# Weight blocks of two tiles: all high-part products before the low-part products

## Chip, cores and metric

The kernel runs on one core of one Trainium2 chip. The metric is the time of one execution on the device in microseconds (us); lower is better, and the output must match the reference.

## The reference

One layer of a hybrid network on 256 tokens of width 2048, with fp32 inputs. `rmsnorm(x)` is multiplied by `w_in` (7440 columns). Of the result, 4112 columns feed a gated delta rule (causal convolution, chunks, a triangular solve) and 3328 feed an RWKV-7 recurrence. Their outputs go through `w_out` and are added to `h`. Then come a cross-attention over 256 memory tokens and a squared-ReLU MLP of hidden width 8192:

```python
h = x
u = rmsnorm(h, mix_norm_w[l]);  p = u @ w_in[l]
o_dn = deltanet_group(p[..., :DN_COLS], ...)
o_rw = rwkv7_group(p[..., DN_COLS:], ...)
h = h + jnp.concatenate([o_dn, o_rw], axis=-1) @ w_out[l]
h = h + memory_cross_attention(rmsnorm(h, xa_norm_w[l]), rmsnorm(mem, mem_norm_w[l]), ...)
h = h + squared_relu_mlp(rmsnorm(h, ffn_norm_w[l]), ffn_w1[l], ffn_w2[l])
return rmsnorm(h, final_norm_w)
```

## The kernel before

Every large product is made from fp32 operands that are split in two parts, a high part rounded to fp32r and the rest as a low part. Three of the four partial products are summed in PSUM: high by high, low activation by high weight, high activation by low weight.

`weights` (L228) loads one block of weights of 512 KB into a `raw` tile (4 buffers) through the SP queue, and splits it: for each of the two 128-row tiles of the block, ScalarE casts the high part `whi` (L239) and VectorE subtracts for the low part `wlo` (L240, recorded as L110, the line of the helper `tt`). `whi` and `wlo` have three buffers each (`WB = 3`), one tile to a buffer. This code has a raised priority (`tc.high_priority(3000)`), so that it is put ahead of other work.

`gemm` (L244) makes a result of 256 tokens by 512 columns. It holds two accumulators of one PSUM bank each, one for each half of the tokens (`m` = 0, 1); the tag "g" has three banks in all. It loops over the blocks `kb` of two weight tiles `q`. For each tile it issues six matmuls of 512 columns, the activations being the stationary operand: for each `m` the high activation by `whi` (L254) and the low activation by `whi` (L255), then for each `m` the high activation by `wlo` (L257). After the last tile `evac` empties each bank: for the MLP and `w_out` on VectorE, for `w_in` half on ScalarE and half on VectorE.

`gemm` is called for 14 groups of `w_in` columns, for `wk` and `wv` (16 tiles each), 8 times for `w_out` (8 tiles), 4 times for `wo` (4 tiles) and 15 times for `w2` (16 tiles): 576 tiles. `gemm_T` (L262) makes the transposed products with `wq` and `w1`; it uses the same `weights` and buffers, with matmuls at L278 and L281. `gemm_rows` (L205) makes the last 512 columns of `w2`, one token half after the other, with buffers of its own; it keeps all its matmuls of one half in one bank.

The order of the instructions on each engine is not that of the program alone. `TileContext(nc, schedule_with_timeline_sim=True)` plans it: instructions are taken by priority (their place in the program, raised where the code says so) as their inputs and buffers become free on a modelled time line. Until about 700 us the many small fp32 matmuls of the two recurrences and of the attention are mixed among those of `gemm` in this way; from then on the MLP is `gemm_T` and `gemm` in turn.

Of the kernel before, what the change touches and what calls it, by code (L numbers as in the profile page):

```python
# [22 lines left out]
KB = 2  # L23
# [81 lines left out]
def body(ctx, tc, I, out, dbg=None, upto=99):  # L105
    nc = tc.nc
    V, A, G, T = nc.vector, nc.scalar, nc.gpsimd, nc.tensor
# [37 lines left out]
    def bank(tag=None):  # L145

        if tag is None:
            tag = ("s0", "s1", "x")[cnt[0] % 3 if stream[0] is None else stream[0]]
        return ps.tile([P, 512], F32, tag=tag, bufs={"g": 3, "x": 1}.get(tag, 2), name=nm("ps_" + tag))
# [78 lines left out]
    def weights(src, a, b, parts):  # L228

        with tc.high_priority(3000):  # L230
            raw = wp.tile([P, a, b], F32, tag="raw", name=nm("raw"))
            nc.sync.dma_start(out=raw, in_=src)
            res = []
            n = a // parts
            for q in range(parts):
                hi = wp.tile([P, n, b], F32R, tag="whi", bufs=WB, name=nm("whi"))
                lo = wp.tile([P, n, b], F32R, tag="wlo", bufs=WB, name=nm("wlo"))
                w = raw[:, q * n:(q + 1) * n]
                A.copy(hi, w)  # L239
                tt(lo, w, hi.bitcast(F32), ALU.subtract)  # L240
                res += [(hi[:, i], lo[:, i]) for i in range(n)]
        return res

    def gemm(lhs, wblk, n, evac, kbs=None):  # L244

        acc = [bank("g") for _ in range(2)]
        kbs = list(kbs if kbs is not None else range(NKT // KB))
        for kb in kbs:
            w = weights(wblk[kb], KB, n, KB)
            for q in range(KB):  # L250
                first, last = kb == kbs[0] and q == 0, kb == kbs[-1] and q == KB - 1
                for m in range(2):
                    xh, xl = lhs(kb * KB + q, m)
                    T.matmul(acc[m][:, :n], lhsT=xh, rhs=w[q][0], start=first, stop=False)  # L254
                    T.matmul(acc[m][:, :n], lhsT=xl, rhs=w[q][0], start=False, stop=False)  # L255
                for m in range(2):
                    T.matmul(acc[m][:, :n], lhsT=lhs(kb * KB + q, m)[0], rhs=w[q][1], start=False, stop=last)  # L257
                    if last:
                        evac(m, acc[m][:, :n])
# [132 lines left out]
    acc = []  # L392
# [6 lines left out]
    with tc.manual_schedule(engines={mybir.EngineType.Activation, mybir.EngineType.DVE}):  # L399
        for kb in range(NKT // KB):  # L400
# [5 lines left out]
            for m in range(2):  # L406
                for q in range(KB):
                    first, last = kb == 0 and q == 0, kb == NKT // KB - 1 and q == KB - 1
                    xh, xo = xl(kb * KB + q, m)
# [3 lines left out]
        for j in range(4):  # L413
# [4 lines left out]
            for m in range(2):  # L418
                T.matmul(ssb[:, 4 * m + j:4 * m + j + 1], lhsT=xs[:, m * P:(m + 1) * P], rhs=ones[:, 0:1],
                         start=True, stop=True)  # L420
# [363 lines left out]
    def win_group():  # L784
        pt = pts()
        gemm(xl, I["w_in"][gi[0]], NB, evac_tok(rx, pt))
        gi[0] += 1
        return pt
# [233 lines left out]
    ptk = pts()  # L1022
    mT = mem_T(lx, "lx")
    gemm(mT, I["wk"][0], NB, evac_tok(rm, ptk))
    to_T(ptk, KT)
    gemm(mT, I["wv"][0], NB, evac_tok(rm, [Vm[:, 0], Vm[:, 1]]))
    for j in range(2):
        split_out(j)
# [92 lines left out]
    for gcol in range(4):  # L1121
        gemm(lambda kt, m: tuple(t[:, m * P:(m + 1) * P] for t in oa[kt]), I["wo"][gcol], NB, add_h(gcol),
             kbs=range(2))
# [70 lines left out]
    for ch in range(4):  # L1194
# [16 lines left out]
        for gcol in range(4):  # L1211
            kbs = range(8 * ch, 8 * ch + 8)
# [26 lines left out]
```

## Time and profile before

| what | us |
|---|---|
| median of 3 runs (1423.86 to 1430.27) | 1428.85 |
| the profiled execution | 1427.91 |
| its span, first to last instruction | 1426.2 |
| TensorE matmul busy (99% of the span) | 1407.6 |
| weight loads busy (82%) | 1172.1 |
| VectorE busy (66%) | 945.7 |
| ScalarE busy (54%) | 776.2 |

PE is TensorE's matmuls, PEld its weight loads, DVE VectorE, ACT ScalarE, POOL GpSimd, SPq and ACTq the queues that issue DMAs. A name like `ps_g<-whi,xhl` says which tile is written from which. A matmul's row is longer than the distance to the next one's start, because matmuls are pipelined and their ends are modelled: a PE that shows no idle time may still have waited a little, and the distance from start to start tells how fast it really goes.

### The profile page before, as it was taken

Reading aid. Unit: us, or ns where it says so; the run is one execution under the profiler, and the core shown is the slowest. Engines: PE = TensorE matmul, PEld = TensorE weight load, DVE = VectorE, ACT = ScalarE, POOL = GpSimd, SP = SyncE. Lnnn points to the kernel's source line nnn. Section 1 sums busy time; section 2 is a strip of 40 time slices with the busy share of each in tenths; the row PEclk is TensorE's granted clock in tenths of the full one; section 3 lists DMA queues with packets and bytes.
Section 4 is the critical chain, followed back from the end, with each engine's and each line's share of the span. In section 5 each row is a group of like instructions: output and inputs, shape, how many; then the busy total and the mean of one; then the engine's idle time right before and its main releaser. Section 6 shows DMA issues by size and latency. Waiting matters only on the chain.

```text
span 1426.2 us, 22860 instructions
## 1 busy us (share of the span) xinstructions
PE 1407.6 (99%) x8308; PEld 1172.1 (82%) x8308; DVE 945.7 (66%) x1788; ACT 776.2 (54%) x1476; POOL 53.0 (4%) x66
## 2 busy tenths in 40 slices
PE   9999999999999999999999999999999999999997
PEld 7877888788887878888788888888888888888886
DVE  7748563858688685766776555665556665566664
ACT  7655554455556454556765544555445544455553
POOL 0010001010010000000000000000000000000000
PEclk9999999999999999999999999999999999999999
DMA  7444443454358455555465566555665556655564
GB/s 272 160 154 142 137 130 106 136 195 140 105 186 238 141 170 173 177 177 178 140 200 189 187 191 198 186 187 192 192 193 191 189 188 194 194 185 188 192 192 148
DMA packets 90114, 250.80 MB, mean 176 GB/s; under 512 B 20609, under 2 KB 29329, under 8 KB 89617
## 3 DMA queue, kind: packets, MB, share of 16 engines
q1 hardware_dynamic: 69728, 241.86, 52.3%
q10 hardware_dynamic: 19920, 6.42, 1.9%
q8 instruction: 65, 1.06, 0.3%
q0 software_dynamic: 352, 1.06, 0.2%
q14 instruction: 49, 0.39, 0.1%
HBM read 242.62 MB, written 6.69 MB: 175 GB/s over the span
## 4 chain that ended last, share of the span: by engine, by line
PE 51%; issue 0%; ACT 0%; DVE 0%; POOLq 0%; POOL 0%
PE ps_g L278 17%; PE ps_g L281 9%; PE ps_g L255 8%; PE ps_g L254 8%; PE ps_g L257 8%; PE ps_g L223 0%; PE ps_g L225 0%; PE ps_g L224 0%; PE ps_x L320 0%; PE ps_s L320 0%; PE ps_s L1112 0%; ACT h L122 0%; ACT junk L122 0%; ACT whi L239 0%; POOLq L1235 0%
## 5 line engine op out<-in xcount | busy, mean ns | idle before, releaser
L110 DVE TENSOR_TENSOR wlo<-raw,whi 128x512 fp32r<-128x512 f32 x848 | 582.1, 691 | 366.6 <-ACT whi L239 314.2
L239 ACT CAST whi<-raw 128x512 fp32r<-128x512 f32 x848 | 524.0, 621 | 485.7 <-DVE wlo L110 202.6
L278 PE MATMUL ps_g<-hhl,whi 128*128 128x512 f32 x1088 | 297.3, 395 | 0.0
L254 PE MATMUL ps_g<-whi,xhl 128*128 128x512 f32 x512 | 207.4, 405 | 0.9 <-ACT whi L239 0.6
L278 PEld LDWEIGHTS ps_g<-hhl,whi 128*128 128x128 f32 x1088 | 186.7, 189 | 25.5
L255 PE MATMUL ps_g<-whi,xhl 128*128 128x512 f32 x512 | 204.1, 399 | 0.0
L254 PE MATMUL ps_g<-whi,fhi 128*128 128x512 f32 x480 | 186.8, 389 | 0.0
L255 PE MATMUL ps_g<-whi,flo 128*128 128x512 f32 x480 | 186.8, 389 | 0.0
L281 PEld LDWEIGHTS ps_g<-hhl,wlo 128*128 128x128 f32 x1088 | 166.3, 189 | 22.6
L281 PE MATMUL ps_g<-hhl,wlo 128*128 128x256 f32 x1088 | 172.9, 281 | 0.0
L257 PE MATMUL ps_g<-wlo,xhl 128*128 128x512 f32 x512 | 170.4, 405 | 2.1 <-DVE wlo L110 2.1
L257 PE MATMUL ps_g<-wlo,fhi 128*128 128x512 f32 x480 | 151.5, 389 | 0.0
L254 PEld LDWEIGHTS ps_g<-whi,xhl 128*128 128x128 f32 x512 | 97.2, 190 | 23.6 <-issue 1.7
L255 PEld LDWEIGHTS ps_g<-whi,xhl 128*128 128x128 f32 x512 | 97.1, 190 | 21.1 <-issue 2.2
L257 PEld LDWEIGHTS ps_g<-wlo,xhl 128*128 128x128 f32 x512 | 94.3, 190 | 23.8 <-DVE wlo L110 4.5
L255 PEld LDWEIGHTS ps_g<-whi,flo 128*128 128x128 f32 x480 | 90.1, 188 | 18.8
L257 PEld LDWEIGHTS ps_g<-wlo,fhi 128*128 128x128 f32 x480 | 90.1, 188 | 18.7
L254 PEld LDWEIGHTS ps_g<-whi,fhi 128*128 128x128 f32 x480 | 90.1, 188 | 18.5
L113 DVE SCALAR_TENSOR_TENSOR cy<-ps_x,colt,cy 128x255 f32<-128x255 f32 (+2 forms) x72 | 34.2, 475 | 2.8 <-ACT cy L122 2.1
L1205 ACT CAST fhi<-hid 128x256 fp32r<-128x256 f32 x64 | 26.1, 407 | 9.7 <-DVE hid L113 9.4
L113 DVE SCALAR_TENSOR_TENSOR h<-ps_g,rf,h 128x512 f32<-128x512 f32 (+1 forms) x34 | 22.9, 716 | 12.0 <-PE ps_g L225 8.7
L113 DVE SCALAR_TENSOR_TENSOR hid<-hid 128x256 f32<-128x256 f32 x64 | 27.3, 427 | 2.1
(353 smaller groups left out, 1440.2 us busy)
## 6 DMA issues: line engine op xcount, KB each, us to landing
raw<-in_w_dram SPq DMA_DIRECT2D x256, 512.0 KB, 4.2
raw<-in_w_in_dram SPq DMA_DIRECT2D x112, 512.0 KB, 3.5
raw<-in_w_out_dram SPq DMA_DIRECT2D x32, 512.0 KB, 4.3
raw<-in_wk_dram SPq DMA_DIRECT2D x8, 512.0 KB, 3.8
raw<-in_wv_dram SPq DMA_DIRECT2D x8, 512.0 KB, 3.5
raw<-in_wq_dram SPq DMA_DIRECT2D x8, 512.0 KB, 3.8
raw<-in_wo_dram SPq DMA_DIRECT2D x8, 512.0 KB, 3.5
wl<-in_w_lora_dram SPq DMA_DIRECT2D x8, 272.0 KB, 6.3
```

The source lines that it names most:

```text
L110: return (e or V).tensor_tensor(o, a, b, op=op)
L113: return V.scalar_tensor_tensor(o, a, s, b, op0=op0, op1=op1)
L239: A.copy(hi, w)
L254: T.matmul(acc[m][:, :n], lhsT=xh, rhs=w[q][0], start=first, stop=False)
L255: T.matmul(acc[m][:, :n], lhsT=xl, rhs=w[q][0], start=False, stop=False)
L257: T.matmul(acc[m][:, :n], lhsT=lhs(kb * KB + q, m)[0], rhs=w[q][1], start=False, stop=last)
L278: T.matmul(acc, lhsT=w[k][0], rhs=rhs(8 * b + k).rearrange("p a t -> p (a t)"), start=b == 0 and k == 0, stop=False)
L281: T.matmul(acc[:, 0:S], lhsT=w[k][1], rhs=rhs(8 * b + k)[:, 0], start=False, stop=b == 1 and k == 7)
L1205: A.copy(hi[:, j], t)
```

## The change

Within a block of two weight tiles, `gemm` now issues the eight matmuls with the high parts of both tiles first, and then the four with the low parts, the two of one token half after the other. Number and shape of the matmuls are the same; `weights`, `gemm_T` and `gemm_rows` are untouched.

```diff
         for kb in kbs:
             w = weights(wblk[kb], KB, n, KB)
             for q in range(KB):
-                first, last = kb == kbs[0] and q == 0, kb == kbs[-1] and q == KB - 1
                 for m in range(2):
                     xh, xl = lhs(kb * KB + q, m)
-                    T.matmul(acc[m][:, :n], lhsT=xh, rhs=w[q][0], start=first, stop=False)
+                    T.matmul(acc[m][:, :n], lhsT=xh, rhs=w[q][0], start=kb == kbs[0] and q == 0, stop=False)
                     T.matmul(acc[m][:, :n], lhsT=xl, rhs=w[q][0], start=False, stop=False)
-                for m in range(2):
+            for m in range(2):
+                for q in range(KB):
+                    last = kb == kbs[-1] and q == KB - 1
                     T.matmul(acc[m][:, :n], lhsT=lhs(kb * KB + q, m)[0], rhs=w[q][1], start=False, stop=last)
                     if last:
                         evac(m, acc[m][:, :n])
```

## Rows read from the trace of the kernel before

**Rows 1.** The page: busy time, share of the span, instructions of each engine

```profile
PE 1407.6 (99%) x8308; PEld 1172.1 (82%) x8308; DVE 945.7 (66%) x1788; ACT 776.2 (54%) x1476; POOL 53.0 (4%) x66
```

**Rows 2.** Stretches: start:end, length, busy time (instructions) by engine, clock, DMA share, GB/s

```profile
278.00:285.00 7.00, 7.00 (x17) 4.98 (x17) 2.57 (x5) 1.73 (x5) 0.64 (x1) 0.52 0.25 80
...
470.00:473.00 3.00, 3.00 (x39) 1.97 (x37) 0.69 (x1) 0.66 (x2) 0.00 (x0) 0.58 0.32 76
...
800.00:890.00 90.00, 90.00 (x402) 74.65 (x401) 51.92 (x78) 41.57 (x67) 0.00 (x0) 1.00 0.62 193
...
1412.00:1426.20 14.20, 5.46 (x24) 4.16 (x23) 3.49 (x8) 3.58 (x8) 0.99 (x2) 0.83 0.41 148
```

**Rows 3.** PE by line, the costliest group of gemm: count | busy us, mean ns | idle

```profile
L254 PE MATMUL ps_g<-whi,xhl 128*128 128x512 f32 x512 | 207.4, 405 | 0.9 <-ACT whi L239 0.6 <-DVE pt L117 0.3
```

**Rows 4.** Timeline in a product with w2: start, length, instruction, idle before

```profile
1002.45 0.39 PE L254 MATMUL ps_g<-whi,fhi 128*128 128x512 f32 x1
...
1002.67 0.39 PE L255 MATMUL ps_g<-whi,flo 128*128 128x512 f32 x1
...
1003.10 0.62 ACT L239 CAST whi<-raw 128x512 fp32r<-128x512 f32 x1 [0.74 <-DVE wlo L110]
...
1003.75 0.69 DVE L110 TENSOR_TENSOR wlo<-raw,whi 128x512 fp32r<-128x512 f32 x1 [0.67 <-ACT whi L239]
...
1004.71 0.39 PE L254 MATMUL ps_g<-whi,fhi 128*128 128x512 f32 x1
...
1006.07 0.39 PE L254 MATMUL ps_g<-whi,fhi 128*128 128x512 f32 x1
...
1006.98 0.62 PE L257 MATMUL ps_g<-wlo,fhi 128*128 128x512 f32 x2
```

**Rows 5.** Timeline where one product with w2 ends and the next begins

```profile
820.59 0.62 PE L257 MATMUL ps_g<-wlo,fhi 128*128 128x512 f32 x2
...
821.01 1.41 DVE L113 SCALAR_TENSOR_TENSOR h<-ps_g,rf,h 128x512 f32<-128x512 f32 x2 [0.24 <-PE ps_g L257]
821.04 0.39 PE L254 MATMUL ps_g<-whi,fhi 128*128 128x512 f32 x1
...
822.40 0.39 PE L254 MATMUL ps_g<-whi,fhi 128*128 128x512 f32 x1
```

**Rows 6.** PE's waits: line, engine waited for, us in total, times, longest

```profile
PE ps_g L257 <- DVE wlo L110: 2.1, 4, 1.0
...
PE ps_g L254 <- ACT whi L239: 0.8, 2, 0.6
```

**Rows 7.** Timeline around two of these waits, before 700 us

```profile
271.66 0.69 DVE L110 TENSOR_TENSOR wlo<-raw,whi 128x512 fp32r<-128x512 f32 x1
271.78 0.40 PE L255 MATMUL ps_g<-whi,xhl 128*128 128x512 f32 x1
...
272.40 0.73 PE L257 MATMUL ps_g<-wlo,xhl 128*128 128x512 f32 x2 [0.22 <-DVE wlo L110]
...
449.45 1.12 DVE L110 TENSOR_TENSOR xtmp<-x,xhalf 64x512 f32<-64x512 f32 x1
```

**Rows 8.** Timeline of gemm_rows, all matmuls of a token half in one bank

```profile
1409.29 0.39 PE L223 MATMUL ps_g<-lhi,fhi 128*128 128x512 f32 x1
...
1410.46 0.39 PE L223 MATMUL ps_g<-lhi,fhi 128*128 128x512 f32 x1
...
1414.12 0.39 PE L224 MATMUL ps_g<-llo,fhi 128*128 128x512 f32 x1
...
1416.85 0.39 PE L224 MATMUL ps_g<-llo,fhi 128*128 128x512 f32 x1
```

**Rows 9.** Timeline where small fp32 matmuls stand between those of gemm

```profile
37.33 0.47 PE L254 MATMUL ps_g<-whi,xhl 128*128 128x512 f32 x1
37.65 0.39 PE L255 MATMUL ps_g<-whi,xhl 128*128 128x512 f32 x1
```

**Rows 10.** The page: DMA issues, KB each, us to landing

```profile
raw<-in_w_dram SPq DMA_DIRECT2D x256, 512.0 KB, 4.2
```

## The prediction

> **What bounds the kernel now.** I read the shares of the engines first. The matmuls are busy 99% of the span, VectorE 66%, ScalarE 54% [rows 1]. A matmul's row is longer than its turn, so this alone does not say that TensorE is full. The windows say where it might not be: only at the end (after 1412 us, 5.46 of 14.20 us busy) is there a stretch without matmuls, and the change does not touch it, because `gemm_rows` makes the last product. In two stretches the granted clock is low, 0.52 from 278 to 285 us and 0.58 from 470 to 473 us; elsewhere, as from 800 to 890 us, it is 1.00 [rows 2]. Third, the timeline of a product with `w2`: two L254 that stand one tile (six matmuls) apart start at 1004.71 and 1006.07 us, so a matmul of 512 columns takes its turn in 1.36/6 = 0.2267 us, against the 0.39 us that its row is long [rows 4]. It keeps this pace across the end of a product: the six from 821.04 to 822.40 us again take 1.36 us [rows 5]. `gemm` has 576 tiles, 3456 matmuls, of which the costliest group of L254 alone, that of the activations of `w_in`, `wk` and `wv`, counts 512 [rows 3]. They need at least 3456 x 0.2267 = 783 us whatever their order. Last, the waits: PE waits for `wlo` 4 times, 2.1 us in all, and for `whi` twice, 0.8 us [rows 6]. So TensorE sets the time, it is fed nearly without a gap, and the order of its matmuls can win only the gaps.
>
> **What the change does to the feeding.** It adds and removes no instruction and no DMA. What moves is when a tile is wanted and when its buffer is given back.
>
> Before, in the steady state: the last reader of a `whi` tile (L255 at 1002.67, row 0.39 long) ends at 1003.06. ScalarE casts into that buffer at 1003.10 for 0.62 us, VectorE subtracts at 1003.75 for 0.69 us. Three buffers on, this tile's first L254 starts at 1006.07, its first L257 at 1006.98 [rows 4]. The cover is 1006.07 - 1003.72 = 2.35 us for `whi` and 1006.98 - 1004.44 = 2.54 us for `wlo`.
>
> After, I number a block's matmuls 0 to 11 and give each 0.2267 us, and a reader is done 0.39 us after its start. Tile 0 of the block is read as `whi` by 0 to 3, tile 1 by 4 to 7; as `wlo`, tile 0 by 8 and 10, tile 1 by 9 and 11. The third tile after a tile takes its buffer:
> - `whi` of tile 0 is free at 3 x 0.2267 + 0.39 = 1.07 us, recast (0.04 + 0.62) at 1.73, wanted at place 16, 3.63 us. Cover 1.90 us.
> - `whi` of tile 1 is free at 1.98, recast at 2.64, wanted at place 24, 5.44 us. Cover 2.80 us.
> - `wlo` of tile 0 is free at 10 x 0.2267 + 0.39 = 2.66, rewritten (0.04 + 0.69) at 3.39, wanted at place 21, 4.76 us. Cover 1.37 us.
> - `wlo` of tile 1 is free at 2.88, rewritten behind the other one at about 4.1, wanted at place 32, 7.25 us. Cover 3.1 us.
>
> All four stay positive by more than one VectorE instruction of 0.69 us, so in the MLP the change costs nothing. The work that hides it is the pair of ScalarE and VectorE, which need 0.62 and 0.69 us of each 1.36 us. If the cover of 1.37 us were gone, PE would lose what is lacking once per block. Behind the waiting `wlo` on VectorE stand the evacuations and, before 700 us, the recurrences.
>
> The `raw` tile is given back when its second `wlo` is written, now 3.39 us after the start of the block before, against 1.73 + 0.69 = 2.4 us by the old order: one microsecond later. A buffer of four comes round every fourth block, 4 x 2.72 = 10.9 us, and a load lands in 4.2 us [rows 10]. It is hidden; if it weren't, the cast would be late by the difference. I cost it at nothing.
>
> The evacuation of the first half can begin one matmul (0.23 us) earlier. PE lost nothing there before: the evacuation of 1.41 us at 821.01 runs beside an unbroken row of matmuls, which the planner had put in the order L254, L255, L257 of one half while the other bank was still held [rows 5]. No gain.
>
> The waits for `wlo`: at 271.66 VectorE begins the low part that L257 wants at 271.78 + 0.23 = 272.01; it starts at 272.40, 0.39 us late, because VectorE was busy with the recurrence [rows 7]. Now tile 0's L257 come four places (0.91 us) later, tile 1's one place earlier. All four waits, with the 0.16 us that each row's length hides (0.39 - 0.2267), are worth 2.1 + 4 x 0.16 = 2.7 us. Half the tiles are tile 0, so I take half, 1.4 us; the bounds are 0 and 2.7. On the other side tile 1's `whi` is wanted two places (0.45 us) earlier: the waits of 0.8 us may become twice that. I take 0.4 us of loss.
>
> New is that the two low products of one half follow each other in the same bank with another moving tile. No row of `gemm` repeats this as a rule; the nearest is `gemm_rows`, where all matmuls of a half share one bank. There 5 turns from 1409.29 to 1410.46 take 0.234 us each, and 12 turns from 1414.12 to 1416.85 take 0.2275 us [rows 8]. So the price lies between 0 and 0.007 us for 2 matmuls in each of 288 blocks: 0 to 4.0 us. I take 0, since the second stretch has the same succession at the usual pace.
>
> Before 700 us the planner will mix the small matmuls in at other places. The first fp32r matmul after small fp32 ones takes 37.65 - 37.33 = 0.32 us, not 0.23 [rows 9]: ten switches more or fewer are 1 us, of either sign. The stretches at the low clock cost 7.0 x 0.48 + 3.0 x 0.42 = 4.6 us now [rows 2]; both sides are open here too, from all of it won to as much again lost. I take 0.
>
> Sum: 1427.91 (the profiled execution, 1.7 us more than its span) - 1.4 + 0.4 = 1426.9 us. The median of the runs lies 0.9 us above the profiled execution, so the forecast is 1428 us.
>
> **Rivals.**
> 1. *New waits for the low part, slower.* Before 700 us VectorE has other work in its queue, pieces such as one of 1.12 us at 449.45 [rows 7], and tile 1's `wlo` can't be begun before its buffer is free, so its cover falls from 2.54 to 1.37 us. With two such pieces ahead of it, it is late. There are (576 - 240)/2 = 168 blocks outside the MLP. The rival decides when they lose 7 us (0.5%), 0.04 us for each; with 0.5 us in every sixth it is 14 us, 1442 us. Against it: a tile 0 has 0.91 us more, VectorE falls behind mostly for reasons that hold either way, and the planner places low products where it sees them ready. Chance 0.12.
> 2. *The planner makes little of it.* Rows already show an order that is not the program's [rows 5]; if it mixes as before, the time is that of before, 1428 to 1429. Chance 0.10, and it counts as no change.
> 3. *Low clock and waits go, faster.* If the gaps (2.7 us) and the low clock (4.6 us) both vanish, 1428.85 - 7.3 = 1421.5 us, just the border of 0.5%. For it: the low stretches lie among the small matmuls that get mixed anew; against it: nothing in the change thins or thickens those. Chance 0.07.
> 4. *The order changes the pace itself.* The shortest step that a row shows is 0.22 us, from 1002.45 to 1002.67 [rows 4]; if all took that, 3456 x 0.0067 would be 23 us, 1405 us. Against it: the pace is 0.2267 through every kind of step, same moving tile or another, same bank or another [rows 4, 5, 8]. Chance 0.02. The Trainium skill, "TensorE: Matmul & The Clock Gate", section Back-to-back issue gap, gives N/2.4 + 2.5 ns for a warm matmul of N columns, 216 ns at 512; by that 3456 x 0.011 = 38 us would be in hand, 1390 us, an estimate. The trace disagrees with that figure here: its 0.2267 us hold where nothing waits.
>
> **How the numbers follow.** My forecast has 0.69, rival 2 0.10, rivals 1, 3 and 4 0.12, 0.07 and 0.02. A measurement of this kernel tells about 0.5% (7 us) from no change: that is 1421.7 to 1436.0. Forecast and rival 2 fall within it, 0.79; rivals 3 and 4 make faster 0.09; rival 1 makes slower 0.12. The range takes in the bounds (2.7 us of waits and the low clock won on one side; 4.0 us of pace, 4.6 us of clock and the milder part of rival 1 on the other): 1420 to 1438 us.
>
> **What the profile after would show.** The same counts at L254, L255 and at the line of the low products; 0.2267 us a matmul in the MLP; there, eight high products and then four low ones in a row; `wlo` begun later after its cast, the cast less late; few waits for `wlo` below 700 us. The forecast is wrong if PE shows waits for `wlo` in many blocks, if the pace in the MLP leaves 0.2267, or if another stretch at the low clock appears.

## The result, and the profile after

The changed kernel takes 1445.29 us in the median of 4 runs (1437.49 to 1446.2), the kernel before 1429.56 us; the ratio is 1.0106 [1.0068, 1.0144]. Slower by about 1%, where no change was forecast, and outside the range of 1420 to 1438 us. Later runs of the same program with its order written out (q_new, below) give 1.0078 [1.0064, 1.0093], so the loss is between 11 and 16 us. The profiled execution took 1444.44 us, its span is 1442.7 us.

The page of the kernel after: busy time by engine, and the two costliest groups of `gemm` on PE with their idle time (L253, L254 are now the high products, L258 the low ones).

```profile
PE 1413.6 (98%) x8308; PEld 1175.8 (81%) x8308; DVE 932.5 (65%) x1788; ACT 772.6 (54%) x1476; POOL 52.9 (4%) x66
...
L253 PE MATMUL ps_g<-whi,xhl 128*128 128x512 f32 x512 | 209.2, 409 | 5.1 <-ACT whi L239 5.1
...
L258 PE MATMUL ps_g<-wlo,xhl 128*128 128x512 f32 x512 | 155.1, 406 | 6.8 <-DVE wlo L110 6.8
```

Counts and busy times are those of [rows 1, 3], nearly; what is new stands behind the last bar, idle time. The waits of PE say the same:

```profile
PE ps_g L258 <- DVE wlo L110: 6.8, 6, 2.2
PE ps_g L253 <- ACT whi L239: 5.1, 6, 2.1
PE ps_s L538 <- DVE b L533: 2.3, 2, 1.9
```

The forecast for these was about 1 us less than before [rows 6]. They are few and long, and all lie in the part where small matmuls are mixed in. The windows split the span at the first product with `w_out` (546 to 583 us in the profiles of this study). First the kernel after, then the kernel before:

```profile
8.00:568.10 560.10, 542.34 (x3914) 438.00 (x3913) 385.59 (x820) 309.57 (x620) 47.29 (x52) 0.98 0.49 156
568.10:1434.00 865.90, 864.45 (x4371) 732.54 (x4370) 541.16 (x948) 456.37 (x843) 3.58 (x4) 1.00 0.57 186
```

```profile
8.00:550.00 542.00, 535.24 (x3899) 433.51 (x3900) 385.81 (x820) 309.53 (x619) 47.31 (x52) 0.99 0.50 160
550.00:1417.10 867.10, 865.54 (x4387) 733.40 (x4385) 554.40 (x950) 459.89 (x843) 3.57 (x4) 1.00 0.58 185
```

Everything is lost ahead of `w_out`: 18.1 us more there, 1.2 us less behind it. PE's idle time there grew from 542.00 - 535.24 = 6.8 us to 560.10 - 542.34 = 17.8 us, 11.0 us. And four stretches at half the clock replace the two of [rows 2]:

```profile
130.80:137.60 6.80, 6.04 (x19) 4.98 (x19) 6.03 (x15) 2.65 (x6) 0.00 (x0) 0.50 0.46 157
383.30:386.70 3.40, 3.40 (x14) 2.84 (x13) 1.95 (x3) 0.62 (x1) 0.00 (x0) 0.51 0.13 41
455.00:461.80 6.80, 5.75 (x17) 4.11 (x16) 5.94 (x21) 3.46 (x7) 2.71 (x1) 0.50 0.45 152
485.70:489.10 3.40, 3.40 (x70) 2.46 (x69) 2.94 (x10) 0.00 (x0) 2.46 (x2) 0.51 0.50 154
```

At 1.2 instead of 2.4 GHz 20.4 us lose up to 10.2 us, against 4.6 us before. That is 5.6 us more, and 11.0 + 5.6 = 16.6 of the 18.1 us; the rest I leave unassigned.

In the MLP the change does what the prediction said. The timeline in a product with `w2`, after:

```profile
997.57 1.07 PE L258 MATMUL ps_g<-wlo,fhi 128*128 128x512 f32 x4
...
998.29 1.29 DVE L110 TENSOR_TENSOR wlo<-raw,whi 128x512 fp32r<-128x512 f32 x2 [1.09 <-PE ps_g L258]
998.47 0.39 PE L253 MATMUL ps_g<-whi,fhi 128*128 128x512 f32 x1
...
1000.29 1.07 PE L258 MATMUL ps_g<-wlo,fhi 128*128 128x512 f32 x4
```

From one group of four low products to the next is 2.72 us for twelve matmuls, 0.2267 us each as in [rows 4]. The split that begins at 998.29 has its first tile ready at about 998.98 and its reader is the second low product, at 1000.52: a cover of 1.54 us, where 1.37 was worked out. What the view also shows is VectorE idle for 1.09 us until PE gives a `wlo` buffer back. Here that costs nothing: behind `w_out` the kernel after is not slower (865.9 against 867.1 us).

Ahead of `w_out` it is slower. The timeline of the kernel after up to its longest wait for `wlo`:

```profile
109.36 0.39 PE L258 MATMUL ps_g<-wlo,xhl 128*128 128x512 f32 x1
110.11 0.17 DVE L117 TENSOR_SCALAR x<-g 64x8 f32<-64x8 f32 x1 [3.47 <-DMA g<-scr]
...
111.21 0.67 DVE L110 TENSOR_TENSOR wlo<-raw,whi 128x512 fp32r<-128x512 f32 x1
...
111.94 0.50 PE L258 MATMUL ps_g<-wlo,xhl 128*128 128x512 f32 x1 [2.19 <-DVE wlo L110]
```

VectorE stands 3.47 us at an instruction that waits for a DMA round trip of the triangular solve (`inverse`), does a few small steps of it, and only then makes the low part; PE has run dry for 2.19 us. This wait of VectorE is for a transfer, not for a `wlo` buffer. This view alone does not say whether the new order brought that about, or an order drawn by the planner that happens to be worse: SyncE's order moved a little, those of VectorE, ScalarE and TensorE much (823 of 1788, 494 of 1460 and 3087 of 7228 places). That is what most runs were for.

### The profile page after: what moved, and what is told of

The parts are those of the page before. It is cut to its first block, busy times and chain, and to the rows that moved or that the text cites. A ratio compares the mean times of both kernels' runs of the same rounds, so it can differ in the third digit from the quotient of the medians.

```text
span 1442.7 us, 22851 instructions
## 1 busy us (share of the span) xinstructions
PE 1413.6 (98%) x8308; PEld 1175.8 (81%) x8308; DVE 932.5 (65%) x1788; ACT 772.6 (54%) x1476; POOL 52.9 (4%) x66
## 4 chain that ended last, share of the span: by engine, by line
PE 88%; DMA 5%; DVE 4%; issue 1%; ACT 1%; SPq 0%; POOLq 0%; POOL 0%; ACTq 0%; DVEq 0%
PE ps_g L279 18%; PE ps_g L253 17%; PE ps_g L258 16%; PE ps_g L254 16%; PE ps_g L282 9%; PE ps_s L684 2%; DMA g<-scr 1%; DVE wlo L110 1%; PE ps_x L321 1%; DMA mraw<-in_memT_dram 1%; DMA xc<-inv 1%; DMA inv<-x 1%; PE ps_s L321 1%; DVE xtmp L110 1%; PE ps_s L866 0%
## 5 line engine op out<-in xcount | busy, mean ns | idle before, releaser
L110 DVE TENSOR_TENSOR wlo<-raw,whi 128x512 fp32r<-128x512 f32 x848 | 568.3, 689 | 380.4 <-PE ps_g L258 220.7
L253 PE MATMUL ps_g<-whi,xhl 128*128 128x512 f32 x512 | 209.2, 409 | 5.1 <-ACT whi L239 5.1
L254 PE MATMUL ps_g<-whi,xhl 128*128 128x512 f32 x512 | 203.8, 398 | 0.0
L253 PE MATMUL ps_g<-whi,fhi 128*128 128x512 f32 x480 | 186.8, 389 | 0.0
L254 PE MATMUL ps_g<-whi,flo 128*128 128x512 f32 x480 | 186.8, 389 | 0.0
L258 PE MATMUL ps_g<-wlo,xhl 128*128 128x512 f32 x512 | 155.1, 406 | 6.8 <-DVE wlo L110 6.8
L258 PE MATMUL ps_g<-wlo,fhi 128*128 128x512 f32 x480 | 132.7, 389 | 0.0
L253 PEld LDWEIGHTS ps_g<-whi,xhl 128*128 128x128 f32 x512 | 97.8, 191 | 29.8 <-ACT whi L239 8.7
L258 PEld LDWEIGHTS ps_g<-wlo,xhl 128*128 128x128 f32 x512 | 94.4, 190 | 30.1 <-DVE wlo L110 10.7
L254 PEld LDWEIGHTS ps_g<-whi,xhl 128*128 128x128 f32 x512 | 97.4, 190 | 20.1 <-issue 1.5
L258 PEld LDWEIGHTS ps_g<-wlo,fhi 128*128 128x128 f32 x480 | 90.1, 188 | 18.8
L253 PEld LDWEIGHTS ps_g<-whi,fhi 128*128 128x128 f32 x480 | 90.1, 188 | 18.7
L254 PEld LDWEIGHTS ps_g<-whi,flo 128*128 128x128 f32 x480 | 90.1, 188 | 18.6
```

What stands on the lines that cost most here:

```text
L110: return (e or V).tensor_tensor(o, a, b, op=op)
L253: T.matmul(acc[m][:, :n], lhsT=xh, rhs=w[q][0], start=kb == kbs[0] and q == 0, stop=False)
```

## The experiments

Three theories. **Buffers** (the cover; near to rival 1): a `wlo` tile is given back later, so VectorE waits at the split, with the recurrences queued behind it. **Plan**: any change of the program's order makes the planner mix the first 550 us anew, and the draw for this one is worse. **Pace**: the order is slower on TensorE in itself.

**Where: the order in one part of the kernel.** e1_late uses the new order from `w_out` on (the flag is set ahead of the first product with `w_out`), e2_early, with `if not late_[0]`, only in `w_in`, `wk` and `wv`.

```diff
+        if late_[0]:
...
+        else:
...
+    late_[0] = True
```

> The new order only in the products from w_out on (w_out, wo, w2); w_in, wk and wv keep the old order. Theory A (shorter cover: a wlo buffer is given back late, so the casts and subtractions stand behind instructions that wait for a DMA, and only the first 550 us have such waits): no loss, ratio to the kernel before 0.996 to 1.004, about 1428 us, the first w_out product at 550 us as before. Theory B (the new order runs slower in itself wherever it stands): 240 + 80 of the 576 tiles are changed, so about half of the 16 us is lost, 1436 us.

> The new order only in w_in, wk and wv (256 of 576 tiles). Theory A: all of the loss is here, ratio 1.007 to 1.014, first w_out product some 18 us later than before. Theory B: about 7 us of loss, ratio 1.005.

e1_late: 1429.23 us, 1.0006 [0.9988, 1.0023]. e2_early: 1441.65 us, 1.0091 [1.0072, 1.011]. 320 of the 576 tiles take the new order for nothing, so the pace theory falls, and the loss is where the windows put it.

**Buffers, with the plan left free.** The number of `wlo` buffers, from three to four, or to two in e5; then four each for `whi` and `wlo` and three for `raw`.

```diff
-lo = wp.tile([P, n, b], F32R, tag="wlo", bufs=WB, name=nm("wlo"))
+lo = wp.tile([P, n, b], F32R, tag="wlo", bufs=4, name=nm("wlo"))
```

> The changed kernel with four wlo buffers in place of three; whi keeps three. A wlo buffer then comes round every fourth tile, two blocks on, and the cover of the low part goes from 1.37 us to about 3.9 us. Theory A: the waits of the matmuls for wlo fall from 6.8 us to under 2 us and the time comes back to 1424 to 1434 us (ratio under 1.003); what stays are waits for whi. Theory C (the planner's new mixture of small and large matmuls is unlucky, whatever the buffers): the time stays within 1437 to 1447 us.

> The kernel before with four wlo buffers: the control for the run that gave the changed kernel four. The old order already has 2.54 us of cover, now 3.9 us, and its PE waits 2.1 us for wlo. Theory A: 0 to 4 us faster, 1423 to 1429 us. If the buffers themselves cost time (another plan, other addresses), it is slower than 1430 us, and then the 1433 us of the changed kernel with four buffers hold such a cost too.

> The kernel before, in its old order, with two wlo buffers in place of three: the cover of the low part falls from 2.54 us to 2.54 - 1.36 = 1.18 us for every tile, like the worst tile of the changed kernel. Theory A: slower in the first 550 us by at least as much as the change, 1440 to 1455 us, with waits for wlo of 6 us or more; the MLP keeps its pace of 0.2267 us a matmul. Theory C: the order of the matmuls is the cause, so this stays at 1425 to 1433 us.

> The kernel before with four whi and four wlo buffers and three raw ones in place of four (the memory for all four sets is not there): whi too is given a cover of 3.7 us. Theory A: the remaining waits of the first 550 us shrink, 1420 to 1428 us, unless the third raw buffer is now the one that is late (a load lands in about 4 us and three buffers come round in 8.2 us), which would show as ScalarE waiting for raw.

> The changed kernel with four whi, four wlo and three raw buffers. Theory A: whi's cover goes from 1.90 to about 4.4 us as well, so the 2.6 us that PE still waited for whi with four wlo buffers go, 1424 to 1431 us. If the planner's mixture has a cost of its own, 1432 us or more.

| run | order | buffers whi, wlo, raw | us | ratio |
|---|---|---|---|---|
| e3_after_lo4 | new | 3, 4, 4 | 1433.26 | 1.0036 [1.002, 1.0052] |
| e4_before_lo4 | old | 3, 4, 4 | 1431.65 | 1.003 [1.001, 1.0051] |
| e5_before_lo2 | old | 3, 2, 4 | 1455.19 | 1.0192 [1.0164, 1.022] |
| e12_before_44r3 | old | 4, 4, 3 | 1431.04 | 1.002 [1.0003, 1.0037] |
| e13_after_44r3 | new | 4, 4, 3 | 1440.84 | 1.0089 [1.0058, 1.0119] |

With four `wlo` buffers the two orders are 1.6 us apart, and taking one from the old order costs 28 us against the kernel before that ran beside it. That speaks for the buffers; but every one of these programs has a plan of its own, and e13, with as many `wlo` buffers, is slow again. Its raw tiles are one fewer, so it differs in more than one thing. The theory of buffers also missed in e4 and e12, which it had put at 1423 to 1429 and 1420 to 1428 us, and in e13, put at 1424 to 1431 us.

**How far a plan alone carries.** e8 and e9 take the token halves in the other order, which changes no buffer's time (e8 in the old order, e9 in the new). e10 (old) and e11 (new) read the two loads, of `g16` and of `xc`, of `inverse` that close the round trips from the `w_out` array instead of the scratch, so that no load waits for a store; the values of the solve are then not the reference's, the amount of work is the same.

```diff
-                for m in range(2):
+                for m in (1, 0):
...
-        A.dma_start(out=g16[:, 0:256].rearrange("q (r c) -> q r c", c=16), in_=diag(s1))
+        A.dma_start(out=g16[:, 0:256].rearrange("q (r c) -> q r c", c=16), in_=diag(flat_w[0:8 * 16512]))
```

> The kernel before with the second token half ahead of the first in every loop of gemm: buffers are given back at the same places, so the cover stays, but the planner gets another program order and mixes anew. Theory A: within 0.4% of before, 1422 to 1434 us. Theory C (luck of the plan): a change of this kind moves the time by some 10 us either way.

> The changed kernel with the token halves swapped in the same way. Theory A: the loss stays with the new order, 1438 to 1450 us. Theory C: the loss was one plan's, and this one may lie anywhere from 1425 to 1450 us.

> The kernel before, but the two loads in inverse() that bring back what was just written to device memory (g16 and xc) read the same pattern from a weight array instead, so they depend on nothing and land early; the values of the inverse are therefore not the reference's, the rest is unchanged. Theory A: the waits of VectorE and ScalarE for g<-scr and xc<-inv vanish (20 us in all), PE's waits for wlo go below 1.5 us, 1418 to 1428 us.

> The changed kernel with the same two loads replaced, so again the values of the inverse are not the reference's. Theory A: with nothing that waits for a DMA in front of the casts and subtractions, the short cover of 1.37 us is nearly enough: the difference to the kernel before with the same loads falls from 16 us to under 6 us. Theory D (VectorE's own work of up to 1.1 us a piece is what delays wlo, the DMA waits matter little): the difference stays at 12 us or more.

e8: 1452.4 us, 1.014 [1.0082, 1.0199]; e9: 1454.16 us, 1.0185 [1.0153, 1.0217]. Swapping halves, which touches no cover, costs the old order about as much as the change does, or more. Most of that is the granted clock: its mean over e8's four runs is 0.986, against 0.9956 in the runs of the kernel before beside it, which by that difference is an estimated 14 of the 22 us between the mean times. e10: 1437.29 us, 1.0066 [1.0044, 1.0089]; e11: 1432.9 us, 1.0044 [1.0025, 1.0064]: without the round trips the new order is the faster of the two by the median, though the intervals overlap, yet neither beats the kernel before, where the theory of buffers had put e10 at 1418 to 1428 us. In e11 VectorE waits 68.9 us for TensorE at a split, more than the 52.1 us of the kernel after, and 13.5 us in e10: such waits alone are not a loss. Over five pairs whose plans were free, the new order came out at +16, +1.6, +9.8, +1.8 and -4.4 us against the old. A comparison in which the plan moves as well can't settle the cause, whichever way it comes out.

**The plan held.** So the planned order of all five engines was recorded and written into the program as a chain of ordering edges; only PE's order within a block is then changed, on the twelve places that the plan gives to its matmuls. In p_after 34 of the 288 blocks keep the old order, in q_old 33 the new one, since otherwise the held queues would wait in a circle.

```diff
+        for a, b in zip(ins, ins[1:]):
+            tc.add_manual_dep(b, a.name, mybir.DependencyInfo(mybir.DependencyClass.NoSync,
+                                                              mybir.DependencyReason.DATA), reason="plan")
...
+        places = sorted(at[b + i] for i in range(12))
+        old = [order[p] - b for p in places]
+        high = [4 * (i // 6) + i % 6 for i in old if i % 6 < 4]
+        for p, i in zip(places, high + [8, 9, 10, 11]):
+            order[p] = b + i
```

> The kernel of before with the planned order of all five engines written out as it was recorded, so that it can't be redrawn: the same instructions in the same order. Every theory: the time of before within 0.3%, 1424 to 1434 us, with the first w_out product at about 550 us and PE idle for about 7 us up to it. It is there to price the writing-out itself.

> The same written-out order, and within the twelve places of a block on PE's queue the eight high-part products come first and the four low-part products last, in 254 of the 288 blocks (34, most of them the first block of a product, keep the old order, because with every other engine's order held they would wait in a circle). VectorE, ScalarE, GpSimd and SyncE keep before's order exactly. Theory of the redrawn plan (the loss is that the planner, given another program order, mixes the first 550 us differently, with the split standing behind instructions that wait for a transfer): 1424 to 1434 us, within 0.4% of the pinned before. Theory of the shorter cover (the loss is the new order's own: wlo given back late): 1436 us or more, waits of PE for wlo and whi of 8 us or more before the first w_out product.

> The run p_after (plan of before, new order within 254 blocks) with four buffers for wlo in place of three; the queues stay as they were, so nothing is planned anew. Theory of the shorter cover as a matter of buffers (VectorE can't make the next low part because the old one is given back late): half or more of p_after's loss comes back, 1442 us or less, and PE's waits for wlo before the first w_out product fall under 4 us. Theory of places (the split stands at places in VectorE's and ScalarE's queues that were chosen for the old order): a buffer doesn't help, 1450 us or more, waits for wlo as in p_after, 8 us.

> The control of p_after_lo4: the plan of before written out, the old order, and four buffers for wlo. Theory of the shorter cover: the old order has little to get back (PE waits 2.0 us for wlo in the pinned before), so 1425 to 1431 us, within 0.2% of p_before; the fourth buffer is worth 28 us under the new order and at most 3 us under the old. If it is far faster than p_before, the buffer is worth something by itself, whatever the order.

> The counterpart of the run p_after: the planned order of the changed kernel written out for all five engines, and within the twelve places of a block on PE's queue the old order (four high, two low, four high, two low) in 255 of the 288 blocks; 33 blocks, most of them the first of a product, keep the new order for the same reason as there. Theory of the shorter cover (the order costs, by itself, whatever the plan): faster than the changed kernel, 1438 us or less. Theory of the plan (the changed kernel's plan is the worse one, whatever stands in its places): the changed kernel's time, 1441 to 1449 us. A third, that putting any other order into places planned for another costs by itself: slower than the changed kernel, 1450 us or more, as p_after was against p_before.

> The changed kernel with its own planned order written out for all five engines: the same instructions in the same order. Both theories: the time of the changed kernel, 1440 to 1449 us. It is there for a closer interval beside q_old and q_new_lo4.

> q_new with four buffers for wlo, the queues unchanged. Theory of the shorter cover: the buffers' part of the loss comes back, about the time of q_old, 1436 to 1441 us; VectorE's waits for TensorE before a split fall from 52 us to about 25. Theory that on its own plan the changed kernel has only a worse plan: no gain, 1442 to 1449 us. If it reaches 1430 us, the plan has no part in the loss.

| queues held as planned for | old order | old, 4 wlo | new order | new, 4 wlo |
|---|---|---|---|---|
| the kernel before | 1428.33 (p_before), 0.9996 [0.9984, 1.0007] | 1428.37 (p_before_lo4), 1.0 [0.9988, 1.0012] | 1456.18 (p_after), 1.0181 [1.016, 1.0201] | 1428.81 (p_after_lo4), 1.0 [0.999, 1.001] |
| the kernel after | 1438.65 (q_old), 1.0066 [1.0052, 1.0081] | not run | 1440.93 (q_new), 1.0078 [1.0064, 1.0093] | 1436.12 (q_new_lo4), 1.005 [1.0037, 1.0064] |

The first line is the test. Writing the order out costs nothing (p_before). On the same queues the new order costs 28 us, and the plan theory had forecast none. One more `wlo` buffer gives all of it back, and gives the old order nothing. So on this plan the whole loss is the `wlo` buffers that come back late. The waits of VectorE between 8 and 550 us show it (engine, line, waited for: us in total, times, longest; these programs have one line for all instructions). p_before, p_after and p_after_lo4:

```profile
DVE wlo L32 <- ACT whi L32: 56.6, 54, 3.1
DVE wlo L32 <- PE ps_g L32: 22.8, 16, 3.3
```

```profile
DVE wlo L32 <- PE ps_g L32: 102.7, 50, 5.3
DVE wlo L32 <- ACT whi L32: 18.5, 15, 3.6
```

```profile
DVE wlo L32 <- ACT whi L32: 58.3, 52, 3.2
DVE wlo L32 <- PE ps_g L32: 16.2, 16, 2.9
```

With three buffers and the new order what ends VectorE's wait at a split is no longer the cast of the high part but TensorE's low product, 50 times, 102.7 us. The longest of these in the timeline of p_after:

```profile
186.77 0.48 DVE L32 SCALAR_TENSOR_TENSOR sh_v<-ps_x,colt,sh_v 128x255 f32<-128x255 f32 x1
...
190.23 0.40 PE L32 MATMUL ps_g<-wlo,xhl 128*128 128x512 f32 x1
190.47 1.00 PE L32 MATMUL ps_s<-r,Sc 128*128 128x64 f32 x8
...
191.72 0.94 PE L32 MATMUL ps_g<-wlo,xhl 128*128 128x512 f32 x3
...
192.53 0.69 DVE L32 TENSOR_TENSOR wlo<-raw,whi 128x512 fp32r<-128x512 f32 x1 [5.28 <-PE ps_g L32]
...
193.53 0.41 DVE L32 TENSOR_TENSOR ze<-ps_s,nsg 128x256 f32<-128x256 f32 x1
...
194.00 0.43 PE L32 MATMUL ps_s<-ze,Sc 128*128 128x64 f32 x2 [0.80 <-DVE ze L32]
```

The four low products of a block no longer run in a row: the first at 190.23, then small matmuls of the recurrence, then three from 191.72. VectorE idles 5.28 us for the buffer, `ze` of the recurrence stands behind the split, and TensorE waits for `ze`, not for `wlo`. So part of the price appears under other names: ahead of `w_out`, TensorE's waits for `wlo` itself grow by 6.2 us (8.2 against 2.0), its idle time by 13.5 us, as the windows below show. The same step in p_before, where that split had run at 179.57:

```profile
179.57 0.68 DVE L32 TENSOR_TENSOR wlo<-raw,whi 128x512 fp32r<-128x512 f32 x1
...
183.66 0.42 DVE L32 TENSOR_TENSOR ze<-ps_s,nsg 128x256 f32<-128x256 f32 x1 [0.54 <-PE ps_s L32]
...
185.28 0.43 PE L32 MATMUL ps_s<-ze,Sc 128*128 128x64 f32 x2
```

Here VectorE waits for TensorE at `ze`, as it should, and TensorE has no gap. Of the 27.6 us by which p_after's first `w_out` product is later than p_before's (574.1 against 546.5 us), the windows give PE 13.5 us more idle time:

```profile
8.00:574.10 566.10, 545.65 (x3906) 437.74 (x3905) 382.24 (x821) 308.21 (x622) 46.62 (x52) 0.98 0.48 154
```

```profile
8.00:546.50 538.50, 531.50 (x3904) 430.66 (x3903) 386.13 (x820) 310.03 (x620) 46.87 (x52) 1.00 0.50 162
```

(566.10 - 545.65 = 20.5 against 538.50 - 531.50 = 7.0 us), and the clock most of the rest: p_after has 23.5 us at half speed, up to 11.8 us lost, p_before none there. But the profiled p_before is the fastest of its eleven runs (1424.46 us, clock 0.998). Over all runs the mean granted clock is 0.9955 in p_before and 0.9918 in p_after, an estimated 5 of the 27 us between the mean times. Two of p_after's four stretches:

```profile
177.30:184.00 6.70, 6.37 (x28) 6.28 (x29) 2.39 (x7) 1.18 (x3) 0.00 (x0) 0.50 0.39 94
286.50:296.60 10.10, 9.68 (x20) 6.02 (x21) 3.94 (x12) 2.42 (x6) 1.02 (x1) 0.50 0.28 98
```

The second line of the table tells what the planner did. On the plan that it drew for the new order, that order costs 2.3 us over the old one, with intervals that overlap (q_old, q_new). q_old's 1438.65 us lie just above the 1438 that the theory of buffers allowed and below the 1441 of the theory of the plan; that a foreign order in planned places costs by itself, the third expectation, is refuted. The fourth buffer is worth 4.8 us: its slowest run, 1438.51, is faster than the fastest of q_new, 1438.59. VectorE's waits for TensorE at a split go from 51.4 us in q_new to nothing in q_new_lo4:

```profile
DVE wlo L32 <- PE ps_g L32: 51.4, 43, 3.2
```

```profile
DVE wlo L32 <- PE ps_g L32: 0.6, 2, 0.3
...
DVE x L32 <- DMA g<-scr: 15.2, 5, 4.5
DVE b L32 <- DMA xc<-inv: 10.1, 5, 3.2
```

But 7 us stay, 1.005 [1.0037, 1.0064], with no such wait left, and the old order is 10 us slower on this plan than on its own. The two programs with four buffers and the new order tell the same: 1428.81 us on the plan of the kernel before, 1436.12 us on that of the kernel after. So in the kernel as it was changed, the late buffers are the smaller part, 2.3 to 4.8 of 11.6 us, and the plan the larger. (The old order with four buffers was not run on this plan.) Whether the planner bent its plan to the late buffers or only drew a dearer one isn't shown; e8 drew a dear one for a change that touches no buffer.

What the plan costs can be read from the waits of TensorE, in q_new and then in q_new_lo4:

```profile
PE ps_g L32 <- DVE wlo L32: 7.4, 7, 2.1
PE ps_g L32 <- ACT whi L32: 5.0, 6, 1.4
```

```profile
PE ps_g L32 <- DVE wlo L32: 6.5, 5, 1.9
PE ps_g L32 <- ACT whi L32: 2.5, 3, 1.0
```

The fourth buffer ends VectorE's waits for TensorE, yet of TensorE's own waits 9.0 of 12.4 us stay, against 2.9 us in the kernel before [rows 6]. The window of q_new_lo4 ahead of `w_out`:

```profile
8.00:558.20 550.20, 537.45 (x3917) 435.53 (x3916) 385.77 (x822) 310.07 (x621) 47.44 (x52) 0.99 0.50 159
```

TensorE is idle for 550.20 - 537.45 = 12.8 us there, against 6.8 us in the kernel before. Two of its waits in the timeline of q_new_lo4:

```profile
444.12 0.63 ACT L32 ACTIVATE junk<-junk 128x512 f32<-128x512 f32 x1 [0.59 <-DMA junk<-in_mem_dram]
...
444.75 1.12 ACT L32 CAST whi<-raw 128x512 fp32r<-128x512 f32 x2
...
445.41 0.73 PE L32 MATMUL ps_g<-whi,xhl 128*128 128x512 f32 x2 [1.00 <-ACT whi L32]
...
447.22 0.17 DVE L32 TENSOR_SCALAR x<-g 64x8 f32<-64x8 f32 x1 [3.33 <-DMA g<-scr]
...
448.26 0.68 DVE L32 TENSOR_TENSOR wlo<-raw,whi 128x512 fp32r<-128x512 f32 x1
...
448.99 0.73 PE L32 MATMUL ps_g<-wlo,xhl 128*128 128x512 f32 x2 [1.93 <-DVE wlo L32]
```

A split or a cast stands in its queue behind an instruction that waits for a transfer: on VectorE a round trip of `inverse`, on ScalarE a load of the memory tokens. Three of the five waits for `wlo` are of this kind (1.22, 1.93 and 1.71 us); the kernel before has one such, of 1.03 us. VectorE's waits for the round trips come to 25 us here, against 7.0 and 6.0 us in the kernel before. This is read from traces: e10 and e11, which took the round trips away, had plans of their own again, so no run shows what the kernel would take without these waits.

## Why the prediction was wrong

**The steps that failed** are two terms of the sum, both ahead of `w_out`. The larger is "Before 700 us the planner will mix the small matmuls in at other places ... I take 0". It was priced by the switches from small to large matmuls alone, and their number did not change: in the trace before and in the trace after, 150 matmuls into `ps_g` follow one into another tile. What the traces show in its place is TensorE waiting for splits and casts that stand behind instructions which wait for a transfer. Held plans price the redrawn plan: 7 us between the two plans for the new order with four buffers (q_new_lo4 against p_after_lo4), 10 us for the old order with three (q_old against p_before). In e8 a change that touches no buffer cost 24 us by the median, the larger part of it at the low clock. This is the larger lesson on the range: 1420 to 1438 had no room for it.

The smaller is the costing of the waits, and in it the sentence "All four stay positive ... so in the MLP the change costs nothing", which was carried no further than the MLP. The covers were counted in places of 0.2267 us. Ahead of `w_out` a place may hold small matmuls instead, as between 190.23 and 191.72, and the four low products spread over them. There the give-back of `wlo` at the end of a block rather than in its middle can be late by whole microseconds. The prediction wrote down which work stands behind the waiting split, "the recurrences", and gave it no price: it went on to price PE's own waits for `wlo` and `whi`, -1.4 and +0.4 us, while the waits came out at 6.8 and 5.1 us, and PE's idle time at +11 us. By itself this term is worth 28 us on the plan of the kernel before, and 2.3 to 4.8 us on the plan that the changed kernel has.

**Rival 1** had a mechanism that is there, the buffer, the sign and 1442 us, at a chance of 0.12. That its 14 us come near to the loss is luck: on the changed kernel's own plan the buffers account for 2.3 to 4.8 us. Its argument against itself, that tile 0 has 0.91 us more, looks at when the product wants the tile; in p_after it also counts when the product lets it go. Its other argument, that the planner places low products where it sees them ready, fits a loss of 11 to 16 us on a plan drawn for the new order and 28 on one that was not, but isn't shown by that.

**Rival 2**, that the planner makes little of it, is refuted.

**The low clock** was taken as 0 between 4.6 us won and 4.6 lost; up to 5.6 us more were lost in the profiled execution. Rival 3 wanted it gone together with the gaps; both grew.

**What held.** The MLP: pace, succession of banks, covers, `raw` and evacuations cost nothing (865.9 us against 867.1 behind `w_out`; e1_late 1.0006). Rival 4, another pace, is refuted: 0.2267 us in both. The 216 ns that the Trainium skill gives ("TensorE: Matmul & The Clock Gate", section Back-to-back issue gap) as the gap of an isolated warm matmul of 512 columns are not reached in this order either. Of the signs that were to make the forecast wrong, further stretches at the low clock appeared; waits for `wlo` in many blocks did not: they are six against four, and longer.

## What to carry to other kernels

Count a reordering at both ends of a buffer: when it is wanted, and when its last reader gives it back; and price the second by what stands behind the refilling instruction on its engine, in the densest stage, not in the steady one. Look as well at what stands ahead of the refilling instruction: a wait for a transfer there delays it whatever its buffers do. Where a planner orders the queues, a change of the program is two changes; hold the plan, change one thing, and only then believe a pair of times. An order that gives a buffer back later may need one buffer more; old and new order, three and four buffers, on one plan, tell that in four programs.

## What was not expected of the hardware

In the profiled executions the half-speed stretches took up to a third of the loss in the change and over 40% of it in p_after; by the clocks of all runs it is less, about 2 of 12 us between q_new and the kernel before beside it and 5 of 27 us between p_after and p_before (estimates). The same clock is most of the spread within one kernel: p_before's run at 1424.46 us was granted 0.998, its runs above 1430 us 0.993 to 0.994.

Two of the four stretches of the kernel after begin about 1 us behind a gap on TensorE: 1.92 us up to 129.88 and half speed from 130.8, 2.08 us up to 454.04 and half speed from 455.0. Not always: 2.19 us up to 111.94 in the same execution were followed by none, and in the 10 us ahead of the other two, at 383.3 and 485.7, TensorE has no wait above 0.3 us. Where the one does bring the other, the half speed comes on top of the gap, and a sum of waits is then less than their price.
